# A decoder layer on one core: roots on GpSimd, a residual added by DMA, and a rearranged last stage

## The chip, the cores and the metric

The kernel runs on one core of one Trainium2 chip. The metric is the device time of one execution in microseconds. The engines are named as the profile names them: PE (TensorE, with PEld for its weight loads), DVE (VectorE), ACT (ScalarE), POOL (GpSimd) and SP (SyncE, which here only issues DMAs). A queue with a q behind it (SPq, POOLq) is the engine's sequencer.

## The reference

One decoder layer on x of 2048 tokens by 1024 channels, float32, batch 1:

```python
h = rmsnorm(x, g_mix) * (1 + sc_m) + sh_m            # the sc, sh, gt come from silu(c) @ w_ada + b_ada
q, k, v, f_logit, u = split(h @ w_in)
attn = rmsnorm(forgetting_attention(q, k, v, log_sigmoid(f_logit + b)), g_attn_out)
ssm  = rmsnorm(s5_ssm(u, ...), g_ssm_out)
x = x + gt_m * (concat(attn, ssm) @ w_out)           # this x is called x1 below
h = rmsnorm(x, g_ffn) * (1 + sc_f) + sh_f
gate, val = split(h @ w_up)                          # 2 x 2816 columns
y = (silu(causal_dwconv(gate)) * val) @ w_down       # 2816 -> 1024
x = x + gt_f * y
return rmsnorm(x, g_final)
```

`rmsnorm` divides by the root of the mean of squares plus 1e-6, over channels.

## The kernel before, in words

The 2048 tokens are cut into four blocks of 512, numbered 0 to 3. Activations lie with channels on the partitions and tokens along the row, so a tile is 128 channels by 512 tokens. Every float32 product is made of three matmuls: each operand is split into a high part (rounded by ACT's CAST) and a low part (the rest, a DVE subtraction), and high x high, high x low and low x high are added up in PSUM. `weights.split` does it for weights: a raw tile is loaded by SP, ACT writes the high part and DVE the low part.

The stages follow each other in time: the input projection with the state-space part (to about 600 us), attention, output projection and the MLP of blocks 0 and 1 (to about 1900 us), then blocks 2 and 3 together. For these two, the up projection (`up_pair`) and most of the down projection are done with seven block products in place of eight, for a pair of blocks, a pair of row groups and a pair of column groups at a time (kinds b11, b21, t1, t2, b22, t3, t4). The operands of the down projection wait in DRAM (`op_d`, `act_d`) and are fetched ahead.

The order of the instructions on each engine is written by a planner when the kernel is built: it simulates the program with costs of its own and puts each engine's instructions in the order in which they come up, with those under `tc.high_priority()` first. On the chip each engine takes its queue strictly in that order, and waits on semaphores. `tc.issue_after(ins)` holds instructions behind another one on the same engine.

**Reciprocal roots.** `rsqrt_mean` (L172) gets sums of squares, one column for each 128 tokens, and returns one over the root of their mean: one DVE instruction makes `rs_v`, two make a first guess from the bits, and three rounds of three refine it, twelve DVE instructions in all on 128 x 4 (or 128 x 2) numbers. It is called 21 times. Around it, `token_sums` (L352) sums over channels by matmuls with a column of ones, and `over_channels` (L358) spreads the result over the partitions by transposes.

**The down projection of blocks 2 and 3** is `down_both`. Its results stand in sixteen tiles `y[b][d]` (`yt` in the profile; b is the block, d the group of 128 output channels). Three parts follow each other. The first takes the row groups FIRST and writes y. The second, JOINT, takes three groups g = 0, 1, 2 of 2, 3 and 3 row-group pairs; in each it goes over four pairs dp of output channels (d1 = 2 dp, d2 = 2 dp + 1), makes the seven products and adds them into y (`add`, L1524). The third takes the row groups LAST (four of them) for one output d at a time: eight outputs of block 2, four of block 3, and then the last four of block 3 in two halves p of 256 tokens.

`want` puts a tile to fetch into a list, `fill` issues the fetches on SP as long as there are free slots (27 in three pools, used in turn), and `done(n)` gives n slots back. In the last group the list holds eight tiles of x1 (two channel groups each, L1498), and behind them the eight tiles of LAST's activations (L1500). x1 is added into y by DVE (`add_x1`, L1556): four adds after each of the last three pairs of the last group, and four in the last part. `fetch` loads the raw weights of the next pair (L1474).

In the third part the weights of each output are loaded and split for block 2, and loaded and split again for block 3; there the last four are kept in tiles of the ring (`own`) since both halves use them. The squares of the results are taken by ACT and summed by DVE into `sq` (L344). `norm_of(2, ...)` makes block 2's factor; the eight products with it and the eight output DMAs (L1681, L1683) are put into the program just ahead of the two halves (`norm_late[0](range(8))`). `finish_last` (L1689) ends each half of block 3: sums, root, spread, a copy `rb`, and eight products, some on DVE (L1705), some as a scaling on ACT and a product on POOL (L1702, L1703), and eight output DMAs on SP's queue (L1707).

POOL does little: the first constants, sixteen stores of tables (L779, L780) up to 270 us, a few memsets, weight sums in `up_pair` from 2000 us to 2342 us, and the products in `finish_last`.

Of the kernel before, what the change touches and what calls it, by code (L numbers as in the profile page):

```python
# [12 lines left out]
F32 = mybir.dt.float32  # L13
# [9 lines left out]
P = 128  # L23
# [13 lines left out]
RSQRT_MAGIC = float(0x5F3759DF)  # L37
# [83 lines left out]
def hybrid_layer(ctx, tc, x, c_t, w_ada, b_col, gains, w_flat, bf_row, a_re, a_im, log_dt,  # L121
# [24 lines left out]
    G.memset(ones, 1.0)  # L146
    sel = const.tile([P, 2], F32, name="sel")
# [24 lines left out]
    def rsqrt_mean(ss, n, width):  # L172

        v = small.tile([P, 8], F32, name="rs_v")[:, :n]
        V.tensor_scalar(out=v, in0=ss, scalar1=1.0 / width, scalar2=EPS, op0=ALU.mult, op1=ALU.add)
        i = small.tile([P, 8], I32, name="rs_i")[:, :n]
        V.tensor_scalar(out=i, in0=v.bitcast(I32), scalar1=1, scalar2=None, op0=ALU.logical_shift_right)
        V.tensor_scalar(out=i, in0=i, scalar1=-1.0, scalar2=RSQRT_MAGIC, op0=ALU.mult, op1=ALU.add)
        y = i.bitcast(F32)
        for _ in range(3):  # L180
            t = small.tile([P, 8], F32, name="rs_t")[:, :n]
            r = small.tile([P, 8], F32, name="rs_y")[:, :n]
            V.tensor_tensor(out=t, in0=y, in1=y, op=ALU.mult)
            V.scalar_tensor_tensor(out=t, in0=t, scalar=-0.5, in1=v, op0=ALU.mult, op1=ALU.mult)
            V.scalar_tensor_tensor(out=r, in0=t, scalar=1.5, in1=y, op0=ALU.add, op1=ALU.mult)
            y = r
        return y
# [1268 lines left out]
    def down_both(ap, rp, dps, misc):  # L1456
# [98 lines left out]
        def add_x1(b, d):  # L1555
            V.tensor_tensor(out=y[b][d], in0=y[b][d], in1=x1[b % 2 * 4 + d // 2][d % 2].bitcast(F32), op=ALU.add)  # L1556

        last, x1 = {b: [] for b in (2, 3)}, []
        for g, js in enumerate(JOINT):
# [80 lines left out]
        n = len(LAST)  # L1640
# [286 lines left out]
```

## Time and profile before

| | |
|---|---|
| median of 3 runs | 2625.82 us (2625.49 to 2627.09) |
| the profiled execution, span | 2625.8 us |
| PE busy | 2539.7 us (97%) |
| DVE busy | 2043.4 us (78%) |
| ACT busy | 1257.6 us (48%) |
| POOL busy | 145.9 us (6%) |
| DMA | 516.37 MB, 197 GB/s in the mean |
| TensorE clock granted, mean | 0.980 |

A row of the timeline gives the start and the duration in microseconds, the engine, the line of the kernel, the operation, output <- inputs, shapes and count; in brackets the idle time of the engine just before, and what ended it. Matmuls are pipelined: a row's duration overlaps the next one's, and a 512-column matmul of a full stretch starts about 0.23 us after the one before. A row by stretch gives busy time (and count) for each engine, then the granted clock, the mean busy share of the 16 DMA engines, and what they moved. A row by group gives the count, busy time, the mean duration in ns, and the idle time before with what ended it.

### The profile page before, as it was taken

What the parts mean: (1) busy time and instruction counts of PE and PEld (TensorE: products, weight loads), DVE (VectorE), ACT (ScalarE), POOL (GpSimd) and SP (SyncE); (2) the same over time, 40 slices, a digit from 0 to 9 for tenths busy, and PEclk for the clock granted to TensorE, in tenths of its full rate; (3) what the DMA queues carried; (4) which work ended last, traced back from release to release, by engine and by line L of the source; (5) the groups of instructions that cost most, each with busy time, mean ns of one, the idle gap of its engine ahead of it and who ended that gap; (6) DMA issues with size and microseconds to landing.
All of it is one profiled execution on the core that took longest, in us unless ns stands there. A gap on an engine that the chain in (4) does not pass through costs nothing.

```text
span 2625.8 us, 35861 instructions
## 1 busy us (share of the span) xinstructions
PE 2539.7 (97%) x12235; PEld 2056.0 (78%) x12235; DVE 2043.4 (78%) x3824; ACT 1257.6 (48%) x2120; POOL 145.9 (6%) x130
## 2 busy tenths in 40 slices
PE   6999999998999999999999999999989999999997
PEld 3888877887788787888778888888767888887776
DVE  7989688966887878787877777776589888876777
ACT  3423255644454545455545555556554555543213
POOL 0001000000000000000000000000002333320000
PEclk8899999998999999999999999999999999999998
DMA  9476986667556655556557555556733443447573
GB/s 318 150 250 217 299 263 199 198 190 236 173 190 215 199 184 184 191 178 207 176 196 224 184 171 192 170 182 225 245 103 128 168 153 136 153 144 289 190 277 119
DMA packets 269319, 516.37 MB, mean 197 GB/s; under 512 B 27952, under 2 KB 114864, under 8 KB 269136
## 3 DMA queue, kind: packets, MB, share of 16 engines
q1 hardware_dynamic: 267312, 508.84, 58.4%
q0 software_dynamic: 1280, 4.20, 0.4%
q8 instruction: 97, 1.59, 0.3%
q10 hardware_dynamic: 544, 1.05, 0.1%
q14 instruction: 86, 0.70, 0.1%
HBM read 374.32 MB, written 139.59 MB: 196 GB/s over the span
## 4 chain that ended last, share of the span: by engine, by line
PE 80%; DMA 7%; DVE 7%; issue 2%; ACT 2%; SPq 1%; POOL 0%; DVEq 0%; POOLq 0%; ACTq 0%
PE ff_ps L1258 19%; PE up_x L1382 7%; PE ff_ps L1232 7%; PE up_z L1382 5%; PE up_y L1382 4%; PE ff_ps L1290 3%; PE ff_ps L1292 3%; PE ff_ps L1291 3%; PE o_ps L1018 2%; PE o_ps L1022 2%; DMA wada<-in_w_ada 2%; PE proj_ps L439 2%; PE acc_x L1612 2%; PE vq_ps L472 2%; PE qs_ps L472 2%
## 5 line engine op out<-in xcount | busy, mean ns | idle before, releaser
L86 ACT CAST w_hi<-w_raw 128x1024 fp32r<-128x1024 f32 (+4 forms) x187 | 173.1, 927 | 270.5 <-DMA w_raw<-in_w_flat 71.6
L1258 PE MATMUL ff_ps<-h_lo,w_hi 128*128 128x512 f32 x704 | 279.8, 397 | 0.8 <-DVE h_lo L391 0.8
L1258 PE MATMUL ff_ps<-h_hi,w_lo 128*128 128x512 f32 x704 | 280.0, 398 | 0.0
L1258 PE MATMUL ff_ps<-h_hi,w_hi 128*128 128x512 f32 x704 | 279.8, 399 | 0.0
L87 DVE TENSOR_TENSOR w_lo<-w_raw,w_hi 128x1024 fp32r<-128x1024 f32 (+4 forms) x187 | 199.8, 1069 | 64.4 <-ACT w_hi L86 52.5
L1009 DVE TENSOR_TENSOR pl<-pf,ph 128x512 fp32r<-128x512 f32 (+1 forms) x320 | 194.9, 618 | 19.8 <-ACT ph L1008 17.1
L1008 ACT CAST ph<-pf 128x512 fp32r<-128x512 f32 (+1 forms) x320 | 177.9, 569 | 62.4 <-PE o_ps L1018 56.4
L1017 DVE TENSOR_TENSOR acc<-acc,pf 128x512 f32<-128x512 f32 (+2 forms) x264 | 159.2, 605 | 26.0 <-ACT pf L1007 23.5
L1007 ACT ACTIVATE pf<-sc_ps 128x512 f32<-128x512 f32 (+2 forms) x184 | 98.3, 539 | 123.3 <-PE sc_ps L998 74.7
L1258 PEld LDWEIGHTS ff_ps<-h_lo,w_hi 128*128 128x128 f32 x704 | 133.6, 190 | 29.5 <-DVE h_lo L391 1.1
L1258 PEld LDWEIGHTS ff_ps<-h_hi,w_lo 128*128 128x128 f32 x704 | 133.5, 190 | 28.8
L1258 PEld LDWEIGHTS ff_ps<-h_hi,w_hi 128*128 128x128 f32 x704 | 133.4, 190 | 28.6 <-issue 0.2
L116 ACT CAST w_hi<-w_raw 128x1024 fp32r<-128x1024 f32 (+2 forms) x100 | 96.4, 964 | 103.7 <-PE ff_ps L1232 41.9
L1291 PE MATMUL ff_ps<-act_lo,w_hi 128*128 128x512 f32 x352 | 139.6, 397 | 0.0
L1290 PE MATMUL ff_ps<-act_hi,w_hi 128*128 128x512 f32 x352 | 139.4, 398 | 0.2 <-ACT rt L378 0.2
L1292 PE MATMUL ff_ps<-act_hi,w_lo 128*128 128x512 f32 x352 | 139.4, 397 | 0.0
L959 DVE TENSOR_REDUCE mx<-sc_ps 128x1 f32<-128x512 f32 (+2 forms) x164 | 97.6, 599 | 52.4 <-PE sc_ps L958 25.9
L1018 PE MATMUL o_ps<-ph,vv 128*128 128x512 f32 (+1 forms) x320 | 121.2, 380 | 2.2 <-ACT ph L1008 2.2
L1022 PE MATMUL o_ps<-pl,vv 128*128 128x512 f32 (+2 forms) x312 | 116.2, 375 | 0.9 <-DVE pl L1009 0.9
L1382 PE MATMUL up_x<-hh,w_hi 128*128 128x512 f32 x352 | 112.7, 400 | 3.4 <-ACT hh L387 1.8
L1364 POOL TENSOR_TENSOR s<-v_raw 128x512 f32<-128x512 f32 x18 | 27.7, 1538 | 1518.9 <-DVE w_lo L87 1518.9
L86 ACT CAST w_hi<-s 128x1024 fp32r<-128x1024 f32 (+2 forms) x66 | 62.1, 944 | 81.8 <-DVE s L1583 31.7
(678 smaller groups left out, 6961.1 us busy)
## 6 DMA issues: line engine op xcount, KB each, us to landing
w_raw<-in_w_flat SPq DMA_DIRECT2D x193, 512.0 KB
w_lo<-wlo SPq DMA_DIRECT2D x68, 512.0 KB
wlo<-w_lo SPq DMA_DIRECT2D x52, 512.0 KB
kb<-kb SPq DMA_DIRECT2D x80, 256.0 KB
vv<-v SPq DMA_DIRECT2D x80, 256.0 KB
w_raw<-in_w_flat SPq DMA_DIRECT2D x40, 384.0 KB
w_raw<-in_w_flat SPq DMA_DIRECT2D x40, 320.0 KB
wada<-in_w_ada SPq DMA_DIRECT2D x48, 256.0 KB
```

The costliest lines, as they stand in the source:

```text
L86: nc.scalar.copy(hi[:, :n], raw[:, :n])
L87: nc.vector.tensor_tensor(out=lo[:, :n], in0=raw[:, :n], in1=hi[:, :n].bitcast(F32), op=ALU.subtract)
L1008: A.copy(ph[:, cs], pf[:, cs])
L1009: V.tensor_tensor(out=pl[:, cs], in0=pf[:, cs], in1=ph[:, cs].bitcast(F32), op=ALU.subtract)
L1018: T.matmul(o_ps[:, cs], lhsT=vt[:, i, :], rhs=ph[:, cs], start=first, stop=False)
L1022: T.matmul(o_ps[:, cs], lhsT=vt[:, i, :], rhs=pl[:, cs], start=False, stop=(b > 0 and ch == b - 1 and i == 3))
L1232: mark[0] = T.matmul(ps, lhsT=lt, rhs=rt, start=(i == 0), stop=(i == 23))
L1258: T.matmul(ps, lhsT=lt, rhs=rt, start=(n == 0), stop=(n == 23))
L1290: T.matmul(ps, lhsT=a, rhs=ah[:, ts], start=(c == 0), stop=False)
L1291: T.matmul(ps, lhsT=a, rhs=al[:, ts], start=False, stop=False)
L1292: mark[0] = T.matmul(ps, lhsT=bb, rhs=ah[:, ts], start=False, stop=(c == n - 1))
L1382: mark[0] = T.matmul(ps, lhsT=lt, rhs=rt, start=(first and n == 0), stop=(n == 11), skip_group_check=not first)
```

## The change

Four edits are made together.

1. `rsqrt_mean` makes `rs_v` as before on DVE and then raises it to the power -0.5 in one POOL instruction, with a constant tile `mhalf`.
2. x1 isn't fetched any more. Behind each pair of the second joint group (g = 1), POOL issues four DMAs that add x1 from DRAM into the four y tiles of that pair.
3. In the last part, the weights of each output are loaded and split once, for block 2, into eight tiles of the ring, and block 3 uses the same tiles.
4. Block 2's output products and DMAs are spread over block 3's work: two behind each of the outputs 1, 2 and 3, and one behind each of the outputs 4 and 5 of the first half. In `finish_last`, the square of the last output channel group isn't added by DVE: TensorE sums it beside the rest. In the second half, every other output DMA goes out on ACT's queue.

```diff
+    mhalf = const.tile([P, 8], F32, name="mhalf")
+    G.memset(mhalf, -0.5)
...
         V.tensor_scalar(out=v, in0=ss, scalar1=1.0 / width, scalar2=EPS, op0=ALU.mult, op1=ALU.add)
-        i = small.tile([P, 8], I32, name="rs_i")[:, :n]
-        V.tensor_scalar(out=i, in0=v.bitcast(I32), scalar1=1, scalar2=None, op0=ALU.logical_shift_right)
-        V.tensor_scalar(out=i, in0=i, scalar1=-1.0, scalar2=RSQRT_MAGIC, op0=ALU.mult, op1=ALU.add)
-        y = i.bitcast(F32)
-        for _ in range(3):
...
-        return y
+        r = small.tile([P, 8], F32, name="rs_y")[:, :n]
+        G.tensor_tensor(out=r, in0=v, in1=mhalf[:, :n], op=ALU.pow)
+        return r
...
-        def add_x1(b, d):
-            V.tensor_tensor(out=y[b][d], in0=y[b][d], in1=x1[b % 2 * 4 + d // 2][d % 2].bitcast(F32), op=ALU.add)
...
-                    if b == 2:
-                        for b2 in (2, 3):
-                            for d in range(0, 8, 2):
-                                want(x1_d[b2][d : d + 2], x1)
...
-                if g == len(JOINT) - 1 and dp:
-                    for d in range(4):
-                        add_x1(*((2, d), (2, d + 4), (3, d))[dp - 1])
-
-        done(6)
+                if g == 1:
+                    for b in (2, 3):
+                        for d in (d1, d2):
+                            G.dma_start(out=y[b][d], in_=x1_d[b][d], accum_op=ALU.add)
+
...
             for d in range(8 if b == 2 else 4):
-                w = weights.split(w_cols(LAST[0], n, d), n * P)
+                if b == 2:
+                    t = ap.tile([P, 2, TB], F32R, name="ring", tag="ring", bufs=RINGL)
+                    w.append(weights.split(w_cols(LAST[0], n, d), n * P, t[:, 0], t[:, 1]))
                 ps = bank(next(banks))
-                plain(ps, w, act)
+                plain(ps, w[d], act)
                 add(b, d, ps)
-                if b == 2 and d < 4:
-                    add_x1(3, 4 + d)
                 sum_squares(sq, d == 0, y[b][d], slice(0, TB), V)
+                if b == 3 and d:
+                    norm_late[0]((2 * d - 2, 2 * d - 1))
...
-                own = {}
-                for d in range(4, 8):
-                    t = ap.tile([P, 2, TB], F32R, name="ring", tag="ring", bufs=RINGL)
-                    own[d] = weights.split(w_cols(LAST[0], n, d), n * P, t[:, 0], t[:, 1])
-                norm_late[0](range(8))
                 for p in range(2):
...
-                        plain(ps, own[d], act, ts)
-                        e = add(3, d, ps, ts)
-                        sum_squares(sq, False, y[3][d][:, ts], ts, V)
+                        plain(ps, w[d], act, ts)
+                        add(3, d, ps, ts)
+                        if d < 7:
+                            sum_squares(sq, False, y[3][d][:, ts], ts, V)
+                        if p == 0 and d < 6:
+                            norm_late[0]((d + 2,))
...
+        end = sq_pool[-1].tile([P, TB], F32, name="sq", tag="sq", bufs=2)
+        A.activation(end[:, ts], yt[7][:, ts], AF.Square)
         ps = ps_fn()
-        token_sums(ps, sq, 2 * p, 2)
+        for t in (sq, end):
+            for i in range(2):
+                c = (2 * p + i) * P
+                T.matmul(ps[:, i : i + 1], lhsT=t[:, c : c + P], rhs=ones[:, 0:1], start=(t is sq and i == 0),
+                         stop=(t is end), skip_group_check=True)
...
-            Q.dma_start(out[b, d][:, ts], o)
+            (A if p and d % 2 else Q).dma_start(out[b, d][:, ts], o)
```

More of the change, by code (lines that the diff above doesn't have):

```diff
@@ L36 @@
 WSLOT = 1056
-RSQRT_MAGIC = float(0x5F3759DF)
 MAGIC = 12582912.0
@@ L175, in rsqrt_mean @@
         V.tensor_scalar(out=v, in0=ss, scalar1=1.0 / width, scalar2=EPS, op0=ALU.mult, op1=ALU.add)
-        i = small.tile([P, 8], I32, name="rs_i")[:, :n]
-        V.tensor_scalar(out=i, in0=v.bitcast(I32), scalar1=1, scalar2=None, op0=ALU.logical_shift_right)
-        V.tensor_scalar(out=i, in0=i, scalar1=-1.0, scalar2=RSQRT_MAGIC, op0=ALU.mult, op1=ALU.add)
-        y = i.bitcast(F32)
-        for _ in range(3):
[L181 to L186, printed above, removed]
-        return y
+        r = small.tile([P, 8], F32, name="rs_y")[:, :n]
+        G.tensor_tensor(out=r, in0=v, in1=mhalf[:, :n], op=ALU.pow)
+        return r
     sil = const.tile([P, 8], F32, name="sil")
@@ L1553, in down_both @@
             done(2 * n)
-        def add_x1(b, d):
-            V.tensor_tensor(out=y[b][d], in0=y[b][d], in1=x1[b % 2 * 4 + d // 2][d % 2].bitcast(F32), op=ALU.add)
-        last, x1 = {b: [] for b in (2, 3)}, []
+        last = {b: [] for b in (2, 3)}
         for g, js in enumerate(JOINT):
```

4 lines of the change are left out of this document (2 added, 2 removed).

## The prediction

> **What bounds the kernel now.** I read the page first: how full TensorE is, and where in the span it isn't.
>
> ```profile
> span 2625.8 us, 35861 instructions
> PE 2539.7 (97%) x12235; PEld 2056.0 (78%) x12235; DVE 2043.4 (78%) x3824; ACT 1257.6 (48%) x2120; POOL 145.9 (6%) x130
> PE   6999999998999999999999999999989999999997
> ```
>
> The span, 2625.8 us, equals the median of the runs (2625.82), so sums against the one hold for the other. TensorE is full nearly everywhere; no TensorE work worth counting is removed, so only its stops and the end can give time. Busy time by stretch shows the stops (matmuls in brackets):
>
> ```profile
> core 0: us, PE busy (x) PEld busy (x) DVE busy (x) ACT busy (x) POOL busy (x), PEclk, DMA share, GB/s
> 600.00:1000.00 400.00, 390.70 (x1870) 315.27 (x1870) 312.30 (x582) 200.34 (x334) 1.55 (x3) 0.98 0.60 198
> 1000.00:1400.00 400.00, 396.95 (x1830) 319.02 (x1829) 317.36 (x578) 219.07 (x367) 0.00 (x0) 1.00 0.56 186
> 2460.00:2480.00 20.00, 20.00 (x87) 16.22 (x87) 15.26 (x24) 4.69 (x6) 0.00 (x0) 1.00 0.19 59
> 2499.80:2514.40 14.60, 13.68 (x53) 9.37 (x51) 7.48 (x12) 0.59 (x2) 0.00 (x0) 1.00 1.04 392
> 2530.00:2544.60 14.60, 14.60 (x64) 11.79 (x63) 13.65 (x22) 3.44 (x5) 0.00 (x0) 1.00 0.52 159
> 2562.30:2584.60 22.30, 22.30 (x97) 18.06 (x97) 17.25 (x27) 9.97 (x17) 0.00 (x0) 1.00 0.35 106
> ```
>
> One pair of output channels of a joint group takes 14.6 us and 64 matmuls. The first pair of the last group (from 2499.8) gets 53 into that time, with the DMA engines full: 11 x 14.6/64 = 2.5 us are lost. The stage of the last weights (from 2562.3) has no hole. Then the end, in the timeline:
>
> ```profile
> 2601.43 5.38 DVE L1681 SCALAR_TENSOR_TENSOR yt<-yt,gain,rt 128x512 f32<-128x512 f32 x8
> 2606.42 0.28 PE L1532 MATMUL acc_z<-ring 128*128 128x256 f32 x1
> 2608.24 0.47 DVE L1524 SCALAR_TENSOR_TENSOR yt<-acc_z,mod_tf,yt 128x256 f32<-128x256 f32 x1
> 2610.01 0.40 ACT L343 ACTIVATE sq<-yt 128x256 f32<-128x256 f32 x1
> 2610.55 0.42 DVE L344 TENSOR_TENSOR sq_acc<-sq_acc,sq 128x256 f32<-128x256 f32 x1
> 2612.41 0.85 PE L352 MATMUL misc_ps<-ones,sq_acc 128*128 128x1 f32 x4
> 2613.30 0.16 DVE L175 TENSOR_SCALAR rs_v<-misc_ps 128x2 f32<-128x2 f32 x1 [1.28 <-PE misc_ps L352]
> 2614.11 2.77 POOL L1703 TENSOR_TENSOR yt<-yt,rt 128x256 f32<-128x256 f32 x4 [272.52 <-DVE rs_t L183]
> 2617.72 0.16 DVE L185 SCALAR_TENSOR_TENSOR rs_y<-rs_t,rs_y 128x2 f32<-128x2 f32 x1
> 2618.02 0.66 PE L358 MATMUL misc_ps<-ident,rs_y 128*128 128x128 f32 x2 [4.45 <-DVE rs_y L185]
> 2618.80 0.37 ACT L1698 COPY rt<-misc_ps 128x256 f32<-128x256 f32 x1 [4.81 <-PE misc_ps L358]
> 2619.20 2.05 DVE L1705 SCALAR_TENSOR_TENSOR yt<-yt,gain,misc_ps 128x256 f32<-128x256 f32 x5 [1.33 <-ACT rt L1698]
> 2619.24 2.09 POOL L1703 TENSOR_TENSOR yt<-yt,rt 128x256 f32<-128x256 f32 x3 [2.37 <-ACT rt L1698]
> 2619.71 3.78 SPq L1707 DMA_DIRECT2D out_y<-yt  x8
> ```
>
> The last product ends at 2606.70, the span at 2625.8: a tail of 19.1 us. VectorE makes it: at 2601.43 it takes block 2's eight output products in one piece, 5.38 us, and the adds of block 3's second half queue behind them, so the last add starts 1.5 us after the matmul. The two halves then mix: the second's root is ready at 2617.88, 4.6 us after its first instruction, since the first half's products stand between its steps.
>
> **The tail after the change.** Block 2's products go two at a time behind block 3's sums. From 2585 to 2606.7 VectorE then has 4 x 0.67 + 8 x 0.40 us of adds, some 3.9 of squares and 5.4 of products: 15 of 21 us, so its queue should be short when TensorE ends. The first half ends its products near 2601.0; add, square, sums, root, spread and copy take about 4 us, its four GpSimd products 2.77: GpSimd is free at about 2607.8, and the second half's power is wanted near 2608.9. What is left, by the rows above: add 0.47, square 0.40, sums 0.85 (four matmuls as now; the last channel's square goes to TensorE alone, so the 0.42 of VectorE's add goes), rs_v 0.16, power 0.72, spread 0.66, copy 0.37, outputs 2.09, one DMA issue 0.47 (3.78/8, now on two queues) and the landing 2.3 (2625.8 less 2623.49), with some 0.4 of hand-overs: 8.9 us. **Gain 10.2.**
>
> The power is in no row. GpSimd's rows nearest to it:
>
> ```profile
> L1369 POOL TENSOR_TENSOR s<-w_raw,v_raw 128x512 f32<-128x512 f32 x18 | 39.1, 2173 | 0.0
> L1703 POOL TENSOR_TENSOR yt<-yt,rt 128x256 f32<-128x256 f32 x7 | 4.9, 723 | 274.9 <-DVE rs_t L183 272.5 <-ACT rt L1698 2.4
> L1915 POOL MEMSET const-float32-0.0<- 128x1 f32 x1 | 0.1, 103 | 0.3 <-issue 0.3
> L779 POOL DMA_DIRECT2D tab<-tb_rc x8 | 6.4, 794 | 210.1 <-DVE rs_t L183 161.6 <-DVE tb_rc L645 32.0 <-DVE fg L564 11.6
> tab<-tb_rc POOLq DMA_DIRECT2D x8, 256.0 KB, 4.2
> ```
>
> It lies between 0.10 (the least instruction) and 2.2 us (512 columns). I take 0.72: few columns, but a harder function than a product. The ends move the tail by -0.6 and +1.5. The Trainium skill (GPSIMD Engine Reference, 3.1 Elementwise) gives about 2.6 cycles for an element of a two-input operation; by that 0.55 of L1703's 0.723 us is elements, the fixed part 0.17, and the sum below would be 2616.3. The page has no figure for a power, its section 4.1 keeps elementwise work on VectorE, and it speaks against this edit.
>
> **The roots elsewhere.** 18 of the 21 lie ahead of the last stage. Each loses eleven small VectorE instructions, 0.19 us apart at best: 2.1 us, 38 in all. Where TensorE needs the root:
>
> ```profile
> L185 DVE SCALAR_TENSOR_TENSOR rs_y<-rs_t,rs_y x36: 149/158/164, 18.2 to 1965.9; 128x4 f32<-128x4 f32 x36
> 695.59 0.32 PE L358 MATMUL ff_ps<-ident,rs_y 128*128 128x128 f32 x1 [0.57 <-DVE rs_y L185]
> 1340.84 0.29 PEld L358 LDWEIGHTS ff_ps<-ident,rs_y 128*128 128x128 f32 x2 [0.32 <-DVE rs_y L185]
> 1914.62 0.16 DVE L185 SCALAR_TENSOR_TENSOR rs_y<-rs_t,rs_y 128x4 f32<-128x4 f32 x1
> 1915.08 0.37 PEld L358 LDWEIGHTS ff_ps<-ident,rs_y 128*128 128x128 f32 x2
> ```
>
> It waits twice, 0.57 and 0.32: **-0.9**. The 38 us of VectorE lie beside a TensorE that is 97 to 99% busy (600 to 1400) and count as nothing. But the planner orders all queues anew, and GpSimd joins the chain: by the 9.3 us that TensorE idles from 600 to 1000, half of it either way, I give this term -5 to +5. Behind a power on GpSimd's queue stand only the table stores of the first 270 us, memsets, and (from 2000 on, where no power lies until the end) the weight sums.
>
> **x1 by accumulating DMAs.** Gone: 16 VectorE adds and 16 loads of 256 KB on SP's queue. New: 16 DMAs on GpSimd's queue, issued behind each pair of the second group. A plain 256 KB one costs GpSimd 0.79 us and lands in 4.2. GpSimd is idle there for 272 us. The same outputs are read next four pairs, 58 us, later, so a wait needs a landing ten times as slow. The first twelve run where the DMA engines are free (share 0.19 at 2460). The last four start at about 2500, where they are full:
>
> ```profile
> 2500.58 0.75 DVE L1524 SCALAR_TENSOR_TENSOR yt<-acc_y,mod_tf,yt 128x512 f32<-128x512 f32 x1
> 2508.52 2.29 SPq L1474 DMA_DIRECT2D w_raw<-in_w_flat  x4
> 2511.21 0.33 SPq L1498 DMA_DIRECT2D h_hi<-x  x1
> 2514.33 0.83 ACT L86 CAST w_hi<-w_raw 128x768 fp32r<-128x768 f32 x1 [12.35 <-DMA w_raw<-in_w_flat]
> 2517.01 0.68 DVE L1556 TENSOR_TENSOR yt<-yt,h_hi 128x512 f32<-128x512 f32 x1
> 2521.30 0.50 PE L1612 MATMUL acc_y<-h_hi,w_hi 128*128 128x512 f32 x1 [0.33 <-ACT w_hi L1596]
> ```
>
> The second pair's weights (issued at 2508.5) land at 2514.3, and TensorE waits for them. Taking the x1 loads out does not empty this stretch: the loads of the last four activations stand next in the list, take the same slots at the same place, and are as many bytes (8 x 512 KB for 16 x 256 KB). The last four accumulating DMAs come on top: 1.05 MB at 392 GB/s, 2.7 us later weights: **+2.7**. Ends: 0 if operands outrun them, 5.4 if reading the destination too doubles their time. The Trainium skill (DMA: Bandwidth & Descriptors, Issuing engines are not separate DMA queues) says that DMAs of every issuing engine share the same 16 DMA engines. The full share at 2499.8 is where that would bite; were GpSimd's DMAs free beside SP's, the sum would be 2614.1. Two x1 adds at 2517 stood ahead of weight sums that ScalarE and then TensorE (0.33) waited for: **-0.6**.
>
> **Last weights split once.** Eight loads, casts and subtractions go (0.69 us each on VectorE). TensorE has no hole there, so: 0 by itself; it makes VectorE's room that the tail needs. Its eight tiles come free as the last pair's second, third and fourth products end (after 18 to 36 of its 64 matmuls), 6 to 10 us ahead of the stage; were they late, 2562 would show a hole.
>
> **Sum:** 2625.8 - 10.2 - 0.9 + 2.7 - 0.6 = 2616.8.
>
> **The rivals.** A: as summed, 2612 to 2620.6; 62%. B: the accumulating DMAs cost double in the full stretch and the next pair's weights are late too: 5.4 + 2 in place of 2.7, 2621.5; 9%. For it: share 1.04; against: one pair, and 58 us of room. C: the end doesn't do what it says: block 2's factor comes late, its products stand in VectorE's queue ahead of the adds as now, and only the shorter root (3.6), the second output queue (1.6) and one add (0.4) are won: 2625.8 - 5.6 + 1.2 = 2621.4; 9%. For it: now the factor is there only at 2601; against: most of that was the root between other work. D: VectorE's freed 38 us close holes ahead of 1850: 5 more, 2611.8 and below; 10%. E, slower: the planner prices the power X us below what it takes. TensorE works in order, and its spreads stand close behind the root (0 at 695 and 1340, 0.3 at 1914; 0.1 in the mean). Some six such places and three in the end stop by X each: 9X - 0.6. From X = 1.7 it is over 2631.1, slower by more than 0.2%; at X = 2 it is 2634.2; 10%. For it: no row shows a power; against: GpSimd's whole 256 columns take 0.72.
>
> **How the numbers follow.** 0.2% (5.3 us) is about what a measurement here can tell from no change. Faster: A and D, 0.72; same: B and C, 0.18; slower: E, 0.10. The range, 2607 to 2626, leaves out E and the lower end of D.
>
> **What would show it.** Right: a POOL power under 1 us; the last matmul to the end in 8 to 10 us; output DMAs on two queues; block 2's products no longer in one piece; fewer than 53 matmuls from the last group's start in 14.6 us. Wrong: TensorE waiting at L358 for POOL, a tail over 13 us, or new holes ahead of 1850.

## The result, and the profile after

The kernel became slower: 2640.58 us in the median of 4 runs (2632.36 to 2641.88) against 2625.65 us before; the ratio is 1.0057 [1.0040, 1.0074]. The forecast was 2616.8 us with a range of 2607 to 2626. The profiled execution of the changed kernel is the fastest of its four, 2632.36 us with a span of 2630.7, so the traces show 4.9 us of the difference and not the whole of it.

The page after, its busy time and slices, GpSimd's new instruction, and the DMAs issued by GpSimd (KB each, us to landing):

```profile
span 2630.7 us, 35603 instructions
PE 2531.8 (96%) x12243; PEld 2052.7 (78%) x12243; DVE 2009.0 (76%) x3567; ACT 1250.1 (48%) x2112; POOL 182.9 (7%) x168
PE   6999899999999999999999999999789999999998
...
L178 POOL TENSOR_TENSOR rs_y<-rs_v,mhalf 128x4 f32<-128x4 f32 (+1 forms) x21 | 22.3, 1063 | 1619.8 <-DVE rs_v L176 1539.5
...
yt<-x POOLq DMA_DIRECT2D x16, 256.0 KB, 7.5
...
tab<-tb_rc POOLq DMA_DIRECT2D x8, 256.0 KB, 3.3
```

The slices show where TensorE is less full than before: the 29th (1841 to 1907 us) reads 9 before and 7 now, and the last, with the tail, 7 before and 8 now. VectorE lost 257 instructions and 34 us, and the kernel is slower all the same. The power takes 1.06 us in the mean; an accumulating DMA lands after 7.5 us in the median, and the plain ones of the same size on that queue (table stores, in the first 270 us) after 3.3.

To see where the time went I read four places off the first and last starts of the products: the first up-projection of blocks 2 and 3, the first and the last joint product, the last product of all, and the span's end.

| us, profiled execution | up projection starts | joint stage | last stage | tail | span |
|---|---|---|---|---|---|
| before | 1929.7 | 164.3 | 45.9 | 19.4 | 2625.8 |
| after | 1937.2 | 171.0 | 43.4 | 14.0 | 2630.7 |

The start is 7.5 us later, the joint stage 6.7 longer, the last stage 2.5 and the tail 5.4 shorter; with 1.4 won in between (the up projection) these are the 4.9 us. Part of the second and third number only moved from one stage to the other: 10 products of the last stage start on TensorE ahead of the last joint product in the changed kernel (the first at 2565.45, below), 2 before. These 8 are 1.9 us, so the joint stage itself got 4.8 us longer and the last stage 0.6 shorter.

**Ahead of 1937.** The products of attention (`o_ps`) and the MLP of the first blocks (`ff_ps`), the next stage's first product, and two windows, before:

```profile
L1258 PE MATMUL ff_ps<-h_hi,w_hi x704: 386/393/775, 699.9 to 1792.5; 128*128 128x512 f32 x176
L1018 PE MATMUL o_ps<-ph,vv x320: 275/393/797, 345.0 to 1817.9; 128*128 128x512 f32 x128, 128*128 128x256 f32 x32
L1382 PE MATMUL up_x<-h_hi,w_hi x88: 390/396/498, 1929.7 to 2356.4; 128*128 128x512 f32 x88
1840.00:1870.00 30.00, 27.45 (x132) 22.12 (x131) 19.12 (x59) 15.19 (x25) 0.00 (x0) 1.00 0.70 246
2497.00:2513.60 16.60, 16.13 (x65) 11.63 (x63) 8.48 (x12) 1.35 (x2) 0.00 (x0) 1.00 1.04 396
2560.50:2583.50 23.00, 23.00 (x100) 18.63 (x99) 18.11 (x28) 9.92 (x16) 0.00 (x0) 1.00 0.36 106
```

and the same of the kernel after, with the timeline of the longest stop:

```profile
L1250 PE MATMUL ff_ps<-h_hi,w_hi x704: 387/393/775, 681.6 to 1755.1; 128*128 128x512 f32 x176
L1010 PE MATMUL o_ps<-ph,vv x320: 276/393/587, 342.0 to 1840.6; 128*128 128x512 f32 x128, 128*128 128x256 f32 x32
L1374 PE MATMUL up_x<-h_hi,w_hi x88: 387/393/497, 1937.2 to 2362.6; 128*128 128x512 f32 x88
1840.00:1870.00 30.00, 15.09 (x55) 11.72 (x55) 10.61 (x22) 10.97 (x23) 1.98 (x2) 0.54 0.23 81
2503.20:2525.50 22.30, 19.06 (x65) 12.51 (x63) 10.40 (x16) 1.62 (x3) 2.59 (x3) 0.85 1.06 366
2515.00:2520.00 5.00, 3.37 (x8) 1.83 (x9) 0.75 (x1) 0.00 (x0) 0.00 (x0) 0.66 1.07 352
2516.60:2523.40 6.80, 6.19 (x14) 3.42 (x13) 1.79 (x3) 0.00 (x0) 0.00 (x0) 0.50 1.05 393
2573.30:2596.30 23.00, 23.00 (x103) 19.05 (x102) 14.80 (x22) 6.60 (x11) 0.00 (x0) 1.00 0.07 21
...
1858.85 1.98 POOL L178 TENSOR_TENSOR rs_y<-rs_v,mhalf 128x4 f32<-128x4 f32 x2 [446.48 <-DVE rs_v L176]
1860.52 1.94 PE L1198 MATMUL up_y<-ident,row 128*128 128x128 f32 x8 [8.20 <-DVE row L1194]
...
2513.48 0.73 PE L1597 MATMUL acc_z<-ring,w_hi 128*128 128x512 f32 x2 [0.86 <-DMA ring<-op7b]
2516.02 0.74 PE L1597 MATMUL acc_z<-ring,w_hi 128*128 128x512 f32 x2 [1.59 <-DMA ring<-op8b]
...
2565.45 0.39 PE L1522 MATMUL acc_y<-h_hi,ring 128*128 128x512 f32 x1
```

The last of the 704 MLP products starts 37 us earlier than before and the last product of attention 23 us later. The MLP, and behind it the output projection, is what fills TensorE while attention's last steps wait for each other: from 1840 to 1860 TensorE works on 79 matmuls of the output projection (L1232) before and on none (L1224) after. That cover is now used up, and TensorE stops for 8.20 us at one place, busy 15 of 30 us instead of 27. Two powers (1.98 us) lie inside that stop; the rest of it is the load of rows, ScalarE's squares and VectorE's scaling, which were there before under cover. How much of the loss is the power's own time is told apart below.

**The joint stage.** The first pair of the last group takes 22.3 us in place of 16.6 for the same 65 matmuls. The DMA engines are full in both, but now TensorE waits for operands (`ring`), and after the stops the granted clock is 0.50 from 2516.6 to 2523.4, which makes the 0.66 in the row above it. (The Trainium skill, TensorE: Matmul & The Clock Gate, Part 1: The HAM clock gate, says that the clock falls to half after one idle window of about 3.4 us. The half is what the trace shows; but no stop ahead of it is 3.4 us long: the two longest are 0.86 and 1.59 us, and TensorE was busy 1.54 of the 3.4 us ahead of 2516.6.)

**The tail.** Timeline after:

```profile
2607.52 5.38 DVE L1666 SCALAR_TENSOR_TENSOR yt<-yt,gain,rt 128x512 f32<-128x512 f32 x8
2615.97 0.42 DVE L336 TENSOR_TENSOR sq_acc<-sq_acc,sq 128x256 f32<-128x256 f32 x1
2616.69 0.28 PE L1524 MATMUL acc_z<-ring 128*128 128x256 f32 x1
2616.81 0.50 PE L1683 MATMUL misc_ps<-ones,sq_acc 128*128 128x1 f32 x4
2618.03 0.70 POOL L178 TENSOR_TENSOR rs_y<-rs_v,mhalf 128x2 f32<-128x2 f32 x1 [15.93 <-DVE rs_v L176]
2619.79 2.77 POOL L1694 TENSOR_TENSOR yt<-yt,rt 128x256 f32<-128x256 f32 x4 [1.05 <-ACT rt L1689]
2622.53 0.69 POOL L178 TENSOR_TENSOR rs_y<-rs_v,mhalf 128x2 f32<-128x2 f32 x1
2624.52 2.09 POOL L1694 TENSOR_TENSOR yt<-yt,rt 128x256 f32<-128x256 f32 x3 [1.30 <-ACT rt L1689]
2625.28 2.06 ACTq L1698 DMA_DIRECT2D out_y<-yt  x4
```

Block 2's products still stand in one piece of 5.38 us, and the first half's last square is added only behind it, at 2615.97. The first half's sums come right behind the last product on TensorE, GpSimd's four products for that half end at 2622.56, and only then does the second half's power start, 5.6 us after the last product.

### The profile page after: what moved, and what is told of

Its sections match the earlier page's. It is cut to its first block, busy times and chain, and to the rows that moved or that the text cites. A ratio compares the mean times of both kernels' runs of the same rounds, so it can differ in the third digit from the quotient of the medians.

```text
span 2630.7 us, 35603 instructions
## 1 busy us (share of the span) xinstructions
PE 2531.8 (96%) x12243; PEld 2052.7 (78%) x12243; DVE 2009.0 (76%) x3567; ACT 1250.1 (48%) x2112; POOL 182.9 (7%) x168
## 3 DMA queue, kind: packets, MB, share of 16 engines
q8 instruction: 97, 1.59, 0.3%
## 4 chain that ended last, share of the span: by engine, by line
PE 83%; DMA 7%; DVE 6%; ACT 2%; issue 1%; SPq 1%; POOL 0%; POOLq 0%; DVEq 0%; ACTq 0%
PE ff_ps L1250 19%; PE up_x L1374 7%; PE ff_ps L1224 7%; PE up_z L1374 5%; PE up_y L1374 5%; PE ff_ps L1282 3%; PE ff_ps L1283 3%; PE ff_ps L1284 3%; PE o_ps L1010 2%; PE o_ps L1014 2%; DMA wada<-in_w_ada 2%; PE qs_ps L464 2%; PE proj_ps L431 2%; DMA w_raw<-in_w_flat 2%; PE vq_ps L464 2%; PE acc_x L1597 1%
## 5 line engine op out<-in xcount | busy, mean ns | idle before, releaser
L85 ACT CAST w_hi<-w_raw 128x1024 fp32r<-128x1024 f32 (+4 forms) x175 | 166.0, 949 | 258.5 <-DMA w_raw<-in_w_flat 85.3
L86 DVE TENSOR_TENSOR w_lo<-w_raw,w_hi 128x1024 fp32r<-128x1024 f32 (+4 forms) x175 | 191.6, 1095 | 63.5 <-ACT w_hi L85 56.2
L178 POOL TENSOR_TENSOR rs_y<-rs_v,mhalf 128x4 f32<-128x4 f32 (+1 forms) x21 | 22.3, 1063 | 1619.8 <-DVE rs_v L176 1539.5
L1374 PE MATMUL up_z<-hh,w_hi 128*128 128x512 f32 x308 | 97.6, 398 | 1.9 <-ACT w_hi L85 1.9
```

The source lines that it names most:

```text
L85: nc.scalar.copy(hi[:, :n], raw[:, :n])
L86: nc.vector.tensor_tensor(out=lo[:, :n], in0=raw[:, :n], in1=hi[:, :n].bitcast(F32), op=ALU.subtract)
L1374: mark[0] = T.matmul(ps, lhsT=lt, rhs=rt, start=(first and n == 0), stop=(n == 11), skip_group_check=not first)
```

## The experiments

The theories. **Order theory**: a root that costs the planner something else makes it lay out the first 1900 us anew, and that layout is the loss. **Power theory**: GpSimd's power is late wherever TensorE needs it. **DMA theory**: the accumulating DMAs are the loss. Each ratio below is against the kernel before, run on the same chip. Stage times are read as in the table above.

### The parts alone

Four kernels: the first edit alone (power), the second alone (accumulating DMAs), everything but the power, and everything with the last four accumulating DMAs issued behind the last pair of the last group.

```diff
# everything, last four late
-                if g == 1:
+                if (g == 1 and dp < 3) or (g == 2 and dp == 3):
```

> The kernel before with the first edit alone: all 21 roots by the GpSimd power. Order theory (the power gives the planner another order ahead of 2000 us, which leaves the end of attention uncovered, as in the changed kernel at 1842 to 1870): 7 us lost there, some 3 us won in the last root of the tail, so about 2630. Power theory (the power itself, 1.06 us in the mean, stops TensorE at each spread): 21 waits at the spreads of about 1 us each, about 2640. DMA theory (only the accumulating DMAs cost): about 2623.

> The kernel before with the second edit alone: x1 by 16 accumulating DMAs. The order ahead of 2400 us is that of the kernel before. Order theory: only the full DMA stretch at 2500 to 2530 gets longer, 6 us as in the changed kernel, less the x1 adds: about 2631, with executions within 0.2% of each other. DMA theory: 10 us or more, 2636 and up, and executions 8 us apart as the changed kernel's are. My prediction's own term was +2.1: 2628.

> The changed kernel with the old root: edits 2 to 4 without the power. Order theory: nothing lost ahead of 2400 us, 6 us lost in the DMA stretch, some 3 won in the tail (the output queue, one add, less VectorE work): about 2629. DMA theory: as the changed kernel, about 2638. Power theory: faster than before, about 2622.

> The changed kernel, but the last pair's four accumulating DMAs are issued behind the last pair of the third group (from about 2560 us), where the DMA engines are little used, and not in the full stretch at 2500. If those four DMAs lengthen the full stretch: 6 us less than the changed kernel, about 2626 to 2634 by its two kinds of executions. If the stretch is longer for another reason (the loads of the last activations in place of x1): no change, 2632 to 2641.

| | ratio | up projection starts | joint | last | tail |
|---|---|---|---|---|---|
| power alone | 1.0039 [1.0027, 1.0051] | 1939.0 | 164.0 | 45.9 | 15.6 |
| accumulating DMAs alone | 1.0029 [1.0014, 1.0044] | 1925.4 | 171.7 | 45.8 | 19.7 |
| all but the power | 1.0021 [1.0012, 1.0031] | 1928.7 | 172.4 | 44.5 | 18.7 |
| all, last four late | 1.0052 [1.0035, 1.0068] | 1947.5 | 167.3 | 44.1 | 13.9 |

Edits one and two each lose by themselves, and in different places: the power ahead of 1939 and nowhere else (it wins 3.8 us of tail), the DMAs in the joint stage. No theory that names one of the two alone holds. In the two kernels with the single split, 7 products of the last stage start in the joint stage (2 in the other two), 1.2 us that are not a loss. Moving four DMAs gave 3.7 us of the joint stage back (3.0 without the moved products), but its start was 10 us later than in the changed kernel, whose order is the same up to there: the stretches with full DMA engines (280 to 340 and about 650 us) took that much longer in that execution. So a single profile's start is worth a few us at most, and I use many: the kernel before and all kernels below that keep its roots ahead of the last stage have the same order on TensorE up to the joint stage, and the eleven of them start the up projection between 1922.5 and 1936.3, the middle at 1927.5. With the power in all roots the three starts are 1937.2, 1939.0 and 1947.5.

### Is it the power, or the order?

Power only in the three roots of the last stage; and, with no power at all, one Newton round more or less in the kernel before.

```diff
+    def rsqrt_mean(ss, n, width, late=False):   # late=True in the last three calls
+        if late:
+            G.tensor_tensor(out=r, in0=v, in1=mhalf[:, :n], op=ALU.pow)
...
-        for _ in range(3):
+        for _ in range(4):      # in the other kernel: range(2)
```

> The whole change, but the 18 roots ahead of the last stage keep their VectorE steps; only the three roots of the end are a GpSimd power. Order theory (the early roots' other cost makes the planner lay the first 1900 us out anew, and that layout is the loss): the first up-projection pair starts within 2 us of where it starts before (1929.7), 7 us sooner than after the change; the joint stage still takes 7 us more than before (the accumulating DMAs are all there), the tail 14: near 2625 where before is 2626, so no change that can be told. Power theory (GpSimd's power is slow wherever it stands on the path; most of the loss then sits in the end): as slow as after the change, ratio near 1.005. DMA theory (everything is the accumulating DMAs): still 7 us slower than before less what the end gives, ratio 1.001 to 1.003, and no gain ahead of 1930.

> The kernel before with one Newton round more in all 21 roots: three small VectorE instructions each, no power, no accumulating DMA, end as before. If what matters is VectorE's time: 63 instructions of 0.15 to 0.19 us, nearly all beside a busy TensorE; at most 2 us, and 0.6 of them in the tail: ratio 1.000 to 1.001. Order theory (any other price of the root has the planner lay the queues out anew, and the layouts differ by some us): the start of the first up-projection pair moves by 4 us or more from 1929.7 in either direction, though the instructions added are worth less than 1 us there.

> The kernel before with one Newton round less in all 21 roots (the root is less exact). If VectorE's time and the root's latency set the matter, 63 instructions fewer give what the 63 more cost the other way round: with four rounds the kernel took 1.0067 times as long, so 0.993 to 0.996 here. Order theory (each price of the root makes another layout, and this kernel's order was found at the old price): no such mirror; anything from 0.997 to 1.004, and the start of the first up-projection pair later than the freed instructions explain, or no earlier than 1 us.

Power in the last three alone: 0.9996 [0.9984, 1.0009], start 1924.5, joint 169.7, tail 14.0. The loss ahead of 1930 is gone, as both the order and the power theory allow. Four rounds: **1.0067** [1.0050, 1.0084], start 1946.2; two rounds: 0.9973 [0.9962, 0.9984], start 1921.0. The 63 extra instructions are about 10 us of VectorE's time (0.16 us each), nearly all beside a full TensorE, and the kernel takes 20 us more. TensorE's waits at the spreads of four rounds:

```profile
L358 PE MATMUL ff_ps<-ident,rs_y 128*128 128x128 f32 x36 | 6.9, 319 | 6.2 <-DVE rs_y L185 6.2
```

It waits 6.2 us there against 0.6 before, and the tail is 1.4 longer, so a third of the loss is the longer root itself. The rest I put down to the layout, which differs from the 19th matmul on (the projection for the state-space part, `proj_ps`, for one, ends at 277 us where the eleven have 266 to 272); that share is what is left over, not measured. The time goes the same way with the number of rounds, which I had not expected; but with the power, which is the shortest root of all, it goes the other way. How much of the two-round gain is the root and how much the order stays open.

Then the power in one set of early roots at a time, the rest as before: the 8 roots at the ends of attention and state-space blocks, or the 10 of the other norms.

```diff
# attention                                     # norms: the two calls in norm_sums and norm_factor
-        rs = rsqrt_mean(ss[:, 0:4], 4, 512)
+        rs = rsqrt_mean(ss[:, 0:4], 4, 512, True)
```

> The kernel before with the power in the 8 roots at the ends of attention and state-space blocks alone (two for each block of tokens); all other roots and the end as before. Power theory (GpSimd's power itself is late on the path): 8 of 21 roots, so a third of the loss of the run with the power alone, 3 to 4 us, with TensorE waiting at the spreads for GpSimd. Order theory: TensorE waits less than 1 us for GpSimd in all, and the time is whatever the new layout gives: if the bare stretch at the end of attention (8 us at one place, idle time of 1800 to 2000 over 20 us) comes with it, the start of the first up-projection pair is at 1935 or later and the ratio 1.002 to 1.006; if not, 0.998 to 1.002.

> The kernel before with the power in the roots of the other norms alone (those ahead of the projections and of the MLP), and the old roots at the ends of attention and in the last stage. Power theory: 10 of 21 roots, half of the loss of the run with the power alone, 4 to 5 us, as waits for GpSimd. Order theory: waits for GpSimd under 1 us, and either the bare stretch at the end of attention comes with this set of roots (start at 1935 or later, ratio 1.002 to 1.006) or with the other; if it comes with neither, only the two together make it.

Attention's roots: **0.9978** [0.9968, 0.9989], start 1919.9. The norms' roots: **1.0080** [1.0064, 1.0095], start 1943.2. Of the kernel with power in the norms, a window, the timeline at its longest stop, and TensorE's waits at the spreads:

```profile
1840.00:1870.00 30.00, 13.07 (x51) 8.91 (x50) 16.05 (x49) 13.27 (x28) 0.00 (x0) 0.67 0.39 129
...
1866.33 1.94 PE L1212 MATMUL up_y<-ident,row 128*128 128x128 f32 x8 [9.21 <-DVE row L1208]
...
L364 PE MATMUL ff_ps<-ident,rs_y 128*128 128x128 f32 x36 | 6.2, 295 | 1.0 <-POOL rs_y L180 0.8 <-ACT h_f L1214 0.2
```

The bare end of attention is there (13 of 30 us, a stop of 9.21) with no power within it: GpSimd does nothing in that window, and the roots at that place are the old ones. TensorE waits 0.8 us for the power in all of these spreads. With attention's roots as powers the same window holds 27.85 us of work. So the loss comes with the order and not with the power's own time, and the norms' roots bring that order, which changes TensorE's queue from the start (4 in place of 10 of the conditioning's matmuls stand between the first norm's sums and its spread). Why the planner runs the MLP so much earlier with them stays open, and so does why attention's roots gave a better order than before: both are draws that nobody aimed at. A kernel with the powers in the norms and the old order held fast was not run.

### What of the accumulating DMA costs

The second edit alone with plain DMAs on the same queue, which write x1 over y (the sum of the earlier groups is left out); and, on top of the late power, all sixteen behind the pairs of the last of the three groups.

```diff
-                            G.dma_start(out=y[b][d], in_=x1_d[b][d], accum_op=ALU.add)
+                            G.dma_start(out=y[b][d], in_=x1_d[b][d])
...
-                if g == 1:
+                if g == 2:
```

> The run with the accumulating DMAs alone, but the sixteen are plain DMAs on GpSimd's queue, which write x1 over y instead of adding to it (so the sum of the earlier groups is left out). If the adding is what costs (the destination read too, the landing 7.5 us against 3.3 of a plain one): the joint stage falls from 171.7 to 164 to 167 us, a ratio of 0.999 to 1.001 to the kernel before. If it is the bytes alone that come on top in the full stretch, or the SP list that the x1 loads left: the joint stage stays at 170 to 172 us and the ratio at 1.003. In between: half of each.

> The run with power in the last three roots alone, and besides the 16 accumulating DMAs issued behind the pairs of the third joint group instead of the second. In the second group the last four meet the full DMA engines at 2500; in the third, twelve of the sixteen come while the last group's operands and the last activations are fetched too. Place theory (only the four that fall into the full stretch cost): the joint stage falls from 171 to 165 to 168 us, and the whole is 3 to 6 us faster than the other run, near 2619 to 2622 where before is 2626, ratio 0.997 to 0.999. Bytes theory (an accumulating DMA costs its engines twice wherever it stands, and the loads around it come that much later): all sixteen now fall into a busier stretch, the joint stage takes 173 us or more, ratio 1.001 or above.

Plain: 0.9999 [0.9988, 1.0009], joint stage 165.2. The first pair of the last group and the landing, plain:

```profile
2494.90:2513.10 18.20, 17.29 (x65) 11.31 (x63) 8.48 (x12) 1.35 (x2) 1.51 (x3) 1.00 1.04 396
...
yt<-x POOLq DMA_DIRECT2D x16, 256.0 KB, 4.8
```

and accumulating (second edit alone):

```profile
2495.30:2517.70 22.40, 18.68 (x65) 11.91 (x63) 10.42 (x16) 1.65 (x3) 2.58 (x3) 0.92 1.06 367
...
yt<-x POOLq DMA_DIRECT2D x16, 256.0 KB, 7.2
```

The same bytes from DRAM with no add: the pair takes 18.2 us in place of 22.4 and the DMAs land in 4.8 in place of 7.2. So of the 7.4 us that the joint stage lost, 6.5 go with the adding; the 0.9 that are left for the bytes lie within the 163.7 to 166.6 us that the kernels without accumulating DMAs show. (That GpSimd's DMAs share the 16 engines with SP's, as the Trainium skill says in DMA: Bandwidth & Descriptors, Issuing engines are not separate DMA queues, agrees with the plain ones: 18.2 us for the pair against 16.6 without them.) All sixteen in the last group: 0.9993 [0.9982, 1.0004], joint 171.9. The first pair fell to 19.6 us, the other three rose from 47.2 to 51.0 together: here no place within the last group was free, and only behind its last pair (167.3 above) does the cost fall. There the four land in 4.1 to 5.1 us, where those in the full stretch take 7 to 9.

### The end

The end of the change on the kernel before, with no accumulating DMAs and no single split, and with block 2's products held two behind each add of the first half; the same holding on the kernel with late power; and that with the last four accumulating DMAs late.

```diff
+                        if p == 0:
+                            with tc.issue_after(e.ins):      # e is the add of this output
+                                norm_late[0]((2 * d - 8, 2 * d - 7))
```

> The kernel before with the end of the changed one and no more: power in the last three roots, the last channel's square summed by TensorE, outputs on two queues; x1 loaded and added by VectorE and the last weights split twice as before; and block 2's products held two behind each add of block 3's first half, so that the planner can't put them in one piece. Order theory: the layout ahead of 1930 and the joint stage (164 us) are those of before, and the end gives all it has: the adds no longer stand behind 5.38 us of products, so the tail is 10 to 13 us where before has 19.4, and the whole 6 to 9 us faster, ratio 0.9965 to 0.9980. DMA theory says the same. If VectorE was too full in the last stage without the freed splits and adds, the stage between the joint groups' end and the last product takes 47 to 50 us where before has 45.9, and the ratio is 0.999 or above.

> The run with power in the last three roots alone (accumulating DMAs and the single split as in the change), and block 2's products held two behind each add of block 3's first half. What the piece of 5.38 us costs is then read directly: if the adds behind it were late (the first half's sums came only after the last product), the tail falls from 14.0 to 10 to 12.5 us and the ratio is 0.998 to 0.999. If the piece costs nothing, the tail stays at 14 and the ratio near 1.000. By the prediction's own working the tail is 9.

> The run with held products, and besides the four accumulating DMAs of the last channel pair issued behind that pair in the last joint group, at 2560, instead of at 2500 where the DMA engines are full. Place theory (an accumulating DMA costs only where the DMA engines are full already): the joint stage falls from 170 to 166 or 167 us, the whole 3 to 5 us below the run with held products alone, ratio 0.9965 to 0.998. If their cost comes with them wherever they stand: the same time as that run, with the loss in the last stage, 47 us or more in place of 44.

The end alone: **0.9978** [0.9968, 0.9988]; joint 164.8, last stage 46.0, tail 13.7. Held: 1.0007 [0.9995, 1.0019]; tail 14.1. Held, last four late: **0.9983** [0.9972, 0.9994]; joint 167.3, last stage 44.0, tail 14.4. The piece of 5.38 us is broken up in all three and the tail is 14 us all the same; my expectation of 10 to 13 fell. The timeline of the last of them:

```profile
2600.32 0.41 DVE L350 TENSOR_TENSOR sq_acc<-sq_acc,sq 128x256 f32<-128x256 f32 x1
2601.95 0.28 PE L1538 MATMUL acc_z<-ring 128*128 128x256 f32 x1
2602.07 0.50 PE L1696 MATMUL misc_ps<-ones,sq_acc 128*128 128x1 f32 x4
2605.00 2.77 POOL L1707 TENSOR_TENSOR yt<-yt,rt 128x256 f32<-128x256 f32 x4 [1.01 <-ACT rt L1702]
2607.74 0.69 POOL L180 TENSOR_TENSOR rs_y<-rs_v,mhalf 128x2 f32<-128x2 f32 x1
```

The first half's last square is now added by 2600.73, 1.2 us ahead of the last product, and its sums still come behind that product in TensorE's queue. Next, that product is held behind them, with two or with one of block 2's products behind each add:

```diff
+                        if p and d == 7:
+                            with tc.issue_after(summed[0].ins):   # the first half's last sum
+                                plain(ps, w[d], act, ts)
```

> The run with held products and the last four accumulating DMAs at 2560, and besides the last product of block 3's second half held on TensorE behind the sums of the first half, which so far stood behind that product in TensorE's queue. If that place is what makes the tail 14 us (first half's sums, power, GpSimd's four products of 2.77 us, and only then the second half's power): the tail falls by 1.5 to 3 us, to 11.5 to 13, and the whole to a ratio of 0.997 to 0.998. If the tail is made elsewhere (VectorE's queue, or the output DMAs after the last product), it stays at 14.

> The run with the first half's sums ahead of the last product, but with one of block 2's products behind each of the eight half-width adds instead of two behind each of the first four. If VectorE's queue in the first half is what delays the sums: another 0.5 to 1 us less tail. If the work only moves behind TensorE's last product: 0 to 2 us more tail than that run.

Two: 0.9976 [0.9965, 0.9986], last stage 45.2, tail 12.3. One: 0.9977 [0.9968, 0.9986], 44.9 and 13.2. The tail fell by 2.1 us, but the last stage, which now holds the sums and a short wait for them, grew by 1.2: 0.9 us won in the profiles, too little to tell in the ratios, whose intervals overlap with 0.9983's. In the first of them:

```profile
2597.36 0.58 PE L1700 MATMUL misc_ps<-ones,sq_acc 128*128 128x1 f32 x4
2599.64 0.28 PE L1538 MATMUL acc_z<-ring 128*128 128x256 f32 x1
2599.76 0.38 PE L364 MATMUL misc_ps<-ident,rs_y 128*128 128x128 f32 x2
2600.62 2.77 POOL L1711 TENSOR_TENSOR yt<-yt,rt 128x256 f32<-128x256 f32 x4 [1.26 <-ACT rt L1706]
2603.35 0.70 POOL L180 TENSOR_TENSOR rs_y<-rs_v,mhalf 128x2 f32<-128x2 f32 x1
```

The sums are early, but the spread still comes behind the last product, so the second power waits for GpSimd's four products again, 3.4 us after the last product where the forecast had 2.2.

### What paid, together

Power in attention's roots and the last three, products held, sums first; with the accumulating DMAs (the last four late) and the single split, and without either.

> What paid in the runs, together: power in the attention roots and in the last three (not in the other norms), the last weights split once, accumulating DMAs with the last four at 2560, block 2's products held two behind each add of the first half, the first half's sums ahead of the last product. TensorE's order ahead of the joint stage is that of the run with power in the attention roots. If the gains add (0.9978 and 0.9976): ratio 0.9945 to 0.9965, 9 to 14 us faster than before. If they don't: that of the better one, 0.997 to 0.998.

> The same without accumulating DMAs and without the single split: x1 loaded and added by VectorE, the last weights split twice, as before. If the accumulating DMAs cost something even with the last four at 2560 (3 us of the joint stage): 1 to 3 us faster than the other, ratio 0.994 to 0.996. If VectorE's adds and splits are late in the last stage: 0 to 2 us slower.

**0.9959** [0.9945, 0.9972] with them (2612.56 us against 2621.96), **0.9964** [0.9951, 0.9977] without: both are faster than both kernels, and the gains add. The stages differ and cancel: joint 167.2 and 163.7 (1.2 of the first are moved products of the last stage), last stage 45.3 and 47.8, tail 11.9 and 11.8.

## Why the prediction was wrong

**The roots elsewhere**: the step that turned the sign. It was put at -0.9 with bounds of -5 to +5 for the new order, from the 9.3 us that TensorE idled between 600 and 1000. That is the wrong bound: TensorE's idle time says what a better order could win, not what a worse one can lose. It is +7.5 in the two profiles, 11.5 between the middles of the three starts and the eleven, and 20 us in the median for the norms' roots alone. The working had no term for an order that uncovers steps which run under other work before. The waits for the root itself were as small as said; after the change TensorE's matmuls at the spreads ahead of the last stage have 0.2 us of idle time ahead of them in all, and none of it is put down to the power:

```profile
L350 PE MATMUL ff_ps<-ident,rs_y 128*128 128x128 f32 x36 | 6.1, 291 | 0.2 <-ACT h_f L1200 0.2
```

The price of the power in the tail, 0.72 within 0.10 to 2.2, was right: 0.69 to 0.70 on 128 x 2 (1.06 in the mean of all 21). (By an estimate from the Trainium skill, GPSIMD Engine Reference, 3.1 Elementwise, the fixed part had come out at 0.17 us; on two columns the measured time is four times that.) Rival E had the right sign by a mechanism that did not occur, TensorE stopping at L358 for GpSimd. The sign of a "new hole ahead of 1850" was named and is what the trace shows, a few us behind 1850.

**The accumulating DMAs**: +2.7 with ends 0 and 5.4; the joint stage itself got 4.8 longer in the changed kernel and 7.4 with the second edit alone. The place (mostly the first pair of the last group) and the cause (share of the engines over 1, later operands) were right, the size was not: the term priced the bytes alone, and plain DMAs of the same bytes cost 0.9 and not 7.4. With the adding a DMA lands in 7.2 us where a plain one of the same tensors lands in 4.8, and TensorE then waits for its operands. Rival B had put this at 5.4 + 2, near the larger of the two.

**The tail**: -10.2 forecast, -5.4 measured from the last product's end (19.1 to 13.7). The step that failed is "GpSimd is free at about 2607.8", that is, 1.1 us after the last product: it was to be free before the second half's power is wanted at 2.2 us, but the power started at 5.6 (+3.4). It took the first half's squares to be added right behind its products, some 5 us ahead of the last product, and the sums to follow at once. Two queues made both late: VectorE's, where block 2's products put the last square 0.7 us ahead of the last product (2615.97 against 2616.69), and TensorE's, where the sums stand behind that product. TensorE's queue had them there before, too (they then waited for VectorE as well):

```profile
2607.29 0.58 PE L352 MATMUL misc_ps<-ones,sq_acc 128*128 128x1 f32 x4 [0.59 <-DVE sq_acc L344]
```

That row stood in the timeline and wasn't read. Another 1.3 us is the time from the end of the output products to the span's end, 4.0 us with two queues where 2.8 were taken; what makes it stays open. Rival C came true in its order (one piece, ahead of the adds) and nearly in its price (5.6 against 5.4). But with the piece broken up the tail stayed at 14, so the piece alone was not the cause. A tail over 13 us was named as a sign of being wrong, and it came.

**Last weights split once**: 0 forecast, and nearly right. The stage reads 43.4 to 44.5 us in the kernels that have it against 45.7 to 46.4 with the weights split twice, but most of that is the 5 to 8 products that start earlier, in the joint stage. From the start of the last joint pair to the last product, a stretch that holds them all, it is 60.8 us before and 60.1 after. See below.

**x1's adds**, -0.6, could not be told apart. The sum of the signs, in the profiles: the two terms given to the planner and to the DMAs lost 12.3 us where +1.8 was forecast, and the end won 6.0 where 10.2 was.

## What to carry to other kernels

Where a planner orders the queues, an edit that leaves the work alone but changes one instruction's cost on a path into every stage can be a new draw of the order: try the edit on one group of call sites at a time, and bound it by what the cover is worth (here 12 to 14 us of TensorE in one window of 30), not by the present holes. Price an accumulating DMA by where it falls: in the pair with full DMA engines four of them cost 5.8 us (22.4 against 16.6), four plain ones 1.6. Put it where the DMA engines have room after the last load that something waits for. Before counting a tail, look in each in-order queue at what stands ahead of its first step. Before comparing stages, count what started on the other side of the boundary.

## What the chip showed that I had not expected

A stage without a hole became a little faster. With the weights split once, TensorE works on 103 matmuls in 23.0 us of the last stage where it had 100 before, both 100% busy at a granted clock of 1.00; from one start of a 512-column product to the next it is 0.227 us in the median against 0.232. The share of the DMA engines is 0.07 against 0.36, and VectorE is busy 14.8 us against 18.1. Neither explains the pace. The same stretch of the kernel without the power, and of the one with held products and the last four DMAs late:

```profile
2567.50:2590.50 23.00, 23.00 (x101) 18.70 (x100) 14.27 (x21) 6.86 (x11) 0.00 (x0) 1.00 0.08 24
...
2557.90:2580.90 23.00, 23.00 (x103) 19.05 (x102) 14.32 (x21) 6.82 (x11) 2.53 (x3) 1.00 0.32 58
```

The first has idle DMA engines and little VectorE work and is nearly as slow as before (101), the second has the fast pace at a DMA share of 0.32. What sets it stays open.

In the full pair the DMA engines moved 366 to 367 GB/s with accumulating DMAs and 396 without or with plain ones, at a share of 1.04 to 1.06: so with the adds the same engine time moves fewer bytes.
